# Low parts of attention keys on both partition halves, and compression products filled up with zeros to 128 rows, in a two-layer decoder trunk

## The chip, the cores and the metric

The kernel runs on one core of a Trainium2 chip, as one program. The metric is the time of one execution on the device, in microseconds (us), as the median of a few runs. Names of engines: PE is the tensor engine (PEld its weight loads), DVE the vector engine, ACT the scalar engine, POOL the general engine, SP the one that issues transfers.

## What is computed

The reference is a decoder trunk of two layers on 256 tokens of 1024 features, all in float32. Each layer is a feed-forward block, a block of token mixing, a read of a memory, and a second feed-forward block, each followed by a layer norm. Token mixing runs four mixers on one input projection; two of them, DSA and NSA, are attention of four heads of 64 channels on one shared key head:

```python
def token_mixing(x, w_in, ...):
    parts = jnp.split(x @ w_in, np.cumsum(IN_SPLITS)[:-1].tolist(), axis=-1)
    y_ret, y_dsa, y_nsa, y_ssd = retention(...), dsa_attention(...), nsa_attention(...), ssd_mixer(...)
    gates = jax.nn.sigmoid(br_g.reshape(B, S, N_BRANCH, D))
    merged = jnp.einsum('bsnd,bsnd->bsd', gates, jnp.einsum('bsnw,nwd->bsnd', ys, w_branch))
    return merged @ w_out

# in dsa_attention: one stream of keys; in nsa_attention: two (selected blocks, window)
s = jnp.einsum('bqhd,bqnd->bhqn', qb, ks) * (Dh ** -0.5)
# in nsa_attention, besides: windows of 32 tokens, every 16, compressed to one key and one value each (15 of them)
def compress(t, i):
    blk = t[:, tok] + cmp_pos[i]
    h = jax.nn.gelu(blk.reshape(B, n_cmp, CMP_LEN * Dh) @ cmp_w1[i])
    return h @ cmp_w2[i]
p_cmp = masked_softmax(jnp.einsum('bshd,bcd->bhsc', q, k_cmp) * scale, cmp_visible[None, None])
o_cmp = jnp.einsum('bhsc,bcd->bshd', p_cmp.astype(v_cmp.dtype), v_cmp)
```

## The kernel before

Products are made of two parts for accuracy. A float32 operand is split into a high part that a single pass of the tensor engine carries exactly, and a low part, the remainder; a product is then high by high, high by low and low by high. Weights stream in through SP into buffers named `raw`, ACT makes their high parts `wH` (L177), DVE their low parts `wL` (L178), and PE multiplies (L191 to L193 in `mm3`; L369 and L370 in the feed-forward blocks).

The order of the work on PE is written down by the program: the mixers are Python generators whose small steps are woven between the dense products of the projections, gates and branches (`Weave`, with a fixed rate and fixed shares). So each engine has one fixed sequence of instructions and runs it in order; what differs from run to run is only when each may start.

The attention of DSA and NSA is `attend`. Queries lie in `qT` with 128 rows: the high parts of the 64 channels on partitions 0 to 63, the low parts on 64 to 127. The keys' high parts `keyH` are there twice, on both halves, so that one product over 128 rows gives (high + low query) by high key. The keys' low parts `keyL` lie on the lower half only, and the second product takes the first 64 rows of both. Per head that is

```python
nc.tensor.matmul(r, q, self.keyH[:, kg, :nk], start=i == 0, stop=False, skip_group_check=True)           # L649
nc.tensor.matmul(r, q[:64], self.keyL[:, kg, :nk], start=False, stop=False, skip_group_check=True)       # L650
```

with `nk` = 128 keys for the first 128 queries and 256 for the second. Heads are done four at a time for 128 keys and two at a time for 256, and then one product adds the mask (L654). A maximum by DVE (L657), exponentials by ACT (L660), and a multiplication by POOL (L670) follow, and later transposes on PE (L681), a split of their result by ACT and DVE (`PT`, L207 and L208), and the products with the values (L691, L692).

The compression of NSA has four small float32 products on fewer than 128 rows: L961 (`w2r` by `gx`, rows 0 to 63), L962 (`hrep` by `w2`, rows 64 to 127), and two at L1000 (`vblk` by `pcT`, 64 rows). A float32 product shows as two passes in the trace. `shared_keys` builds `keyH` and `keyL` (L907, L908); `nsa` holds the compression.

Of the kernel before, what the change touches and what calls it, by code (L numbers as in the profile page):

```python
# [9 lines left out]
F32 = mybir.dt.float32  # L10
# [15 lines left out]
# steps of the mixers woven into the dense products, per step of those, and the mixers' shares of them  # L26
# [3 lines left out]
# columns of w_in, as the reference splits them  # L30
# [8 lines left out]
# token-major projection groups, in the order of their columns in the on-chip tile  # L39
# [11 lines left out]
# layout of the weight stream: name -> (offset, floats per partition)  # L51
# [28 lines left out]
# constants that depend on shapes alone  # L80
# [16 lines left out]
def whole(g):  # L97
    """Runs a generator to its end and returns its value."""
    while True:
        try:  # L100
            next(g)
        except StopIteration as e:
            return e.value


class Weave:
    """Weaves chains of small steps into the large products: step() takes the next step of one of them."""
# [18 lines left out]
    def over(self, g, rate):  # L126
        """Runs g, with rate steps of the chains after each of its own."""
# [11 lines left out]
class Trunk:  # L139
# [33 lines left out]
    def split(self, src, n, pool=None):  # L173
        """The exact parts of float32 weights that single-pass products carry."""
# [13 lines left out]
    def mm3(self, out, a, b, start, stop, **kw):  # L188
        """out += a.T @ b in float32 accuracy; a and b are (high, low) pairs."""
        mm = self.nc.tensor.matmul  # L190
        mm(out, a[0], b[0], start=start, stop=False, **kw)  # L191
        mm(out, a[0], b[1], start=False, stop=False, **kw)  # L192
        mm(out, a[1], b[0], start=False, stop=stop, **kw)  # L193
# [16 lines left out]
    def prime(self, g):  # L210
        """Takes a unit of products to its first yield: its weights are loaded and split."""
# [6 lines left out]
    def ahead(self, *key):  # L218
        """A unit that only prepares a chunk of weights."""
# [3 lines left out]
    def run(self, units, then=None, weave=None, rate=0):  # L223
        """Runs units of products; the weights of the next one are prepared ahead of each."""
# [8 lines left out]
    def setup(self):  # L233
# [3 lines left out]
        # the activation table and the tensor engine's clock come up while the first loads run  # L237
# [41 lines left out]
    def later(self, v):  # L279
        """Holds a load into v's tile until the products reach this point: other loads are needed sooner."""  # L280
# [12 lines left out]
    def layer_norm(self, acc, out=None, alone=False):  # L293
# [21 lines left out]
        # the transposes wait for the sums: other products go between them  # L315
        for t in range(2 if out is None else 0):
            for _ in range((2, 5)[t]):
                yield
            if t == 1 and alone:
                # with no other products the tensor engine's clock is kept up  # L320
# [13 lines left out]
    def ffn(self, l, name, wk, dn, hook=None, first=False, then=None, hold=False):  # L334
# [3 lines left out]
        def gu(f):  # L338
            early = f if first else 2
            if early < 2:  # L340
                # the first blocks follow their loads, some input features at a time
# [22 lines left out]
            # a bank each for gate and up: the products with the high parts of x beside those with its low parts  # L364
# [27 lines left out]
        # split: the first unit, for which the caller makes room ahead of the layer norm before it  # L392
# [13 lines left out]
        # the last blocks finish the token tiles one after the other  # L406
# [33 lines left out]
    def kv_unit(self, l, i):  # L440
        """Units 0-3 hold two blocks of key features each, 4-5 and 6-7 a half of the values."""
# [24 lines left out]
    def xattn(self, l, wk, dn, queries, then, apart):  # L466
# [52 lines left out]
        def out(h, n):  # L519
            # the last n heads together  # L520
# [5 lines left out]
        # with products to come under the layer norm the last heads need not finish together  # L526
# [20 lines left out]
    def token_acc(self, acc, blocks, first, last):  # L547
        """Blocks of 2 x 128 input features into all 1024 token-major columns; the last ones a token tile at a time."""
# [34 lines left out]
    def rope(self, n, heads, width, half, tab, mp):  # L583
        """Rotates the first 2 * half of each of the heads' columns, in place, for both token tiles."""
# [13 lines left out]
    def tposes(self, out, srcs, scale=None, eng="act", parts=128):  # L598
        """Up to four [128, <=128] token-major blocks, transposed side by side into out."""
# [8 lines left out]
    def stacked(self, n, mp):  # L608
        """Queries of four heads by token tiles, transposed: the high parts over the low ones."""
# [17 lines left out]
    def values(self, names, mp):  # L627
        """The parts of values by token tiles, side by side."""
# [7 lines left out]
    def attend(self, qT, streams, mask, mp, finish):  # L636
        """Causal attention of four heads on one key head, for streams of keys, values and a scale of their own that are
        added up; mask(t): further 0/1 rows of masked keys. The sums come out with the channels on the partitions."""
        nc = self.nc

        def weights(t, kg, gate, ps):
            """exp(s - max) of four heads, over the sums."""
            nk, hb = 128 * (t + 1), 4 >> t
            sums = self.sm.tile([128, 4], F32, name="s4", tag="s4", bufs=4)
            for h0 in range(0, 4, hb):
                s = self.acc()
                for i in range(hb):
                    q, r = qT[t][:, h0 + i], s[:, i * nk:i * nk + nk]
                    nc.tensor.matmul(r, q, self.keyH[:, kg, :nk], start=i == 0, stop=False, skip_group_check=True)  # L649
                    nc.tensor.matmul(r, q[:64], self.keyL[:, kg, :nk], start=False, stop=False, skip_group_check=True)  # L650
                sv = s[:, :hb * nk].rearrange("p (h k) -> p h k", h=hb)
                # without a mask only the last block of keys has any that come later
# [22 lines left out]
        def products(t, v, ps, first, last):  # L675
# [19 lines left out]
            # the products with the low parts of the values are on the upper half  # L695
# [6 lines left out]
        # the weights of each stream run ahead of the products of the one before  # L702
# [12 lines left out]
    def branch_parts(self, b, y, scale, mp, feat=False):  # L715
        """The transposed parts [128, 2, 256] of y, which is token-major [128, 2, 256] unless feat."""
        nc = self.nc
        # two branches hold their parts at a time
# [705 lines left out]
```

## Time and profile before

| | |
|---|---|
| runs | 1488.06, 1488.38 and 1484.4 us; median 1488.06 us |
| span of the profiled execution | 1484.8 us; no time of its own is recorded beside it |
| PE busy | 1468.4 us, 99% of the span |
| PE weight loads busy | 1298.8 us, 87% |
| DVE, ACT, POOL busy | 1059.2 us (71%), 801.5 us (54%), 124.2 us (8%) |
| mean granted clock of PE | 0.997 of full speed |

The span goes from the first to the last instruction of the program. Busy time is the time in which at least one instruction of the engine is shown as running; matmuls are pipelined and overlap each other in the record, so a row's duration is longer than the step from one product to the next, and it is the steps between starts that add up to the time.

### The profile page before, as it was taken

To read this page: it belongs to the slowest core of one execution; us is meant where nothing else is said; L and a number is where in the kernel's file an instruction comes from. 1 tells how busy PE (TensorE), PEld (TensorE's weight loads), DVE (VectorE), ACT (ScalarE), POOL (GpSimd) and SP (SyncE) were. 2 spreads that over 40 slices of the span, in tenths; PEclk is the share of its full clock that TensorE was granted. 3 is DMA by queue.
4 is the path that set the end of the run, shared out by engine and by line. 5 is a ranking of instruction groups with operands and counts; after the bars stand their busy time and mean duration, and the time that the engine had idled before them with its cause. 6 is when DMAs were issued, how large, how long until landed. Compare 5 with 4: busy or idle time off the path is not lost.

```text
span 1484.8 us, 22612 instructions
## 1 busy us (share of the span) xinstructions
PE 1468.4 (99%) x8949; PEld 1298.8 (87%) x8949; DVE 1059.2 (71%) x1671; ACT 801.5 (54%) x1302; POOL 124.2 (8%) x122
## 2 busy tenths in 40 slices
PE   8999999999999999999999999999999999999997
PEld 6888899899997989888898888898998989888886
DVE  7666668886668777666686566788866688676565
ACT  6555546644554646555545465466445546365552
POOL 0000002201321000000000000023013210000000
PEclk9999999999999999999999999999999999999999
DMA  8576545533345745555556555554433556264550
GB/s 311 194 276 238 185 165 170 173 140 114 117 169 183 262 149 195 202 199 198 198 173 221 193 208 185 174 189 170 143 114 115 175 192 229 100 241 171 204 192 29
DMA packets 40857, 269.38 MB, mean 181 GB/s; under 512 B 4528, under 2 KB 4784, under 8 KB 10288
## 3 DMA queue, kind: packets, MB, share of 16 engines
q1 hardware_dynamic: 40176, 266.89, 50.7%
q8 instruction: 70, 1.15, 0.3%
q10 hardware_dynamic: 576, 1.05, 0.2%
q14 instruction: 35, 0.29, 0.1%
HBM read 266.88 MB, written 1.05 MB: 180 GB/s over the span
## 4 chain that ended last, share of the span: by engine, by line
PE 96%; DVE 1%; DMA 1%; ACT 1%; POOL 0%; issue 0%; DVEq 0%; ACTq 0%
PE tp L369 11%; PE mm L369 11%; PE acc L193 10%; PE acc L191 10%; PE acc L192 10%; PE mm L191 8%; PE mm L192 8%; PE mm L193 8%; PE mm L370 5%; PE tp L370 5%; PE acc L650 1%; PE tp L327 1%; PE acc L649 1%; PE tp L192 1%; PE tp L681 1%; PE tp L193 1%
## 5 line engine op out<-in xcount | busy, mean ns | idle before, releaser
L178 DVE TENSOR_TENSOR wL<-raw,wH 128x1024 fp32r<-128x1024 f32 (+2 forms) x478 | 583.8, 1230 | 240.1 <-ACT wH L177 237.3
L177 ACT ACTIVATE wH<-raw 128x1024 fp32r<-128x1024 f32 (+2 forms) x478 | 496.1, 1048 | 306.7 <-PE mm L192 134.4
L369 PE MATMUL mm<-xP,wH 128*128 128x512 f32 x704 | 249.4, 394 | 1.7 <-DVE xP L208 1.7
L369 PE MATMUL tp<-xP,wH 128*128 128x512 f32 x704 | 249.1, 394 | 0.0
L191 PE MATMUL mm<-xP,wH 128*128 128x256 f32 x736 | 214.5, 291 | 0.3 <-ACT vM L200 0.3
L192 PE MATMUL mm<-xP,wH 128*128 128x256 f32 x736 | 209.0, 284 | 0.0
L193 PE MATMUL mm<-xP,wL 128*128 128x256 f32 x736 | 208.6, 283 | 0.0
L370 PE MATMUL mm<-xP,wL 128*128 128x256 f32 x704 | 195.7, 278 | 0.8 <-DVE wL L178 0.8
L370 PE MATMUL tp<-xP,wL 128*128 128x256 f32 x704 | 195.4, 278 | 0.0
L369 PEld LDWEIGHTS mm<-xP,wH 128*128 128x128 f32 x704 | 132.0, 187 | 33.3 <-ACT wH L177 2.0
L369 PEld LDWEIGHTS tp<-xP,wH 128*128 128x128 f32 x704 | 132.0, 188 | 30.7
L191 PEld LDWEIGHTS mm<-xP,wH 128*128 128x128 f32 x736 | 141.1, 192 | 2.4 <-ACT vM L200 1.4
L192 PEld LDWEIGHTS mm<-xP,wH 128*128 128x128 f32 x736 | 141.2, 192 | 1.3 <-issue 0.6
L193 PEld LDWEIGHTS mm<-xP,wL 128*128 128x128 f32 x736 | 141.1, 192 | 0.1
L192 PE MATMUL acc<-wL,hH 128*128 128x512 f32 x352 | 137.8, 392 | 0.0
L191 PE MATMUL acc<-wH,hH 128*128 128x512 f32 x352 | 137.7, 391 | 0.0
L193 PE MATMUL acc<-wH,hL 128*128 128x512 f32 x352 | 137.5, 391 | 0.0
L370 PEld LDWEIGHTS mm<-xP,wL 128*128 128x128 f32 x704 | 132.2, 188 | 5.3 <-DVE wL L178 1.9
L370 PEld LDWEIGHTS tp<-xP,wL 128*128 128x128 f32 x704 | 132.3, 188 | 0.0
L374 ACT ACTIVATE g<-mm 128x256 f32<-128x256 f32 x88 | 33.8, 384 | 116.6 <-PE mm L370 116.6
L375 DVE TENSOR_TENSOR g<-mm,g 128x256 f32<-128x256 f32 x88 | 37.2, 423 | 78.4 <-ACT g L374 78.3
L193 PE MATMUL acc<-wH,xP 128*128 128x512 f32 (+1 forms) x224 | 85.0, 379 | 1.9 <-POOL xP L1193 1.9
(328 smaller groups left out, 2392.6 us busy)
## 6 DMA issues: line engine op xcount, KB each, us to landing
raw<-in_w_dram SPq DMA_DIRECT2D x232, 1024.0 KB, 4.9
raw<-in_memT_dram SPq DMA_DIRECT2D x5, 1024.0 KB, 4.8
lnG<-in_ln_g_dram SPq DMA_DIRECT2D x8, 512.0 KB, 4.1
lnB<-in_ln_b_dram SPq DMA_DIRECT2D x8, 512.0 KB, 4.8
raw<-in_w_dram SPq DMA_DIRECT2D x4, 624.0 KB, 3.9
w<-in_w_dram SPq DMA_DIRECT2D x8, 256.0 KB, 5.1
raw<-in_xT_dram ACTq DMA_DIRECT2D x4, 256.0 KB, 6.3
raw<-in_w_dram SPq DMA_DIRECT2D x4, 256.0 KB, 6.0
```

The source lines that it names most:

```text
L177: self.nc.scalar.activation(h, src, AF.Copy)
L178: self.nc.vector.tensor_tensor(lo, src, h.bitcast(F32), OP.subtract)
L191: mm(out, a[0], b[0], start=start, stop=False, **kw)
L192: mm(out, a[0], b[1], start=False, stop=False, **kw)
L193: mm(out, a[1], b[0], start=False, stop=stop, **kw)
L327: nc.tensor.transpose(p[:, k * 128:k * 128 + 128], X[:, t, (h * 4 + k) * 128:(h * 4 + k + 1) * 128], self.ident)
L369: nc.tensor.matmul(b[s], w[0][:, off:off + 128], self.xP[:, :, k], start=k == 0, stop=False, skip_group_check=True)
L370: nc.tensor.matmul(b[s][:, :256], w[1][:, off:off + 128], self.xH[:, k], start=False, stop=k == 7, skip_group_check=True)
L374: nc.scalar.activation(g[:, s], b[s][:, 256:], AF.Copy)
L375: nc.vector.tensor_tensor(g[:, s], b[s][:, :256], g[:, s], OP.add)
L649: nc.tensor.matmul(r, q, self.keyH[:, kg, :nk], start=i == 0, stop=False, skip_group_check=True)
L650: nc.tensor.matmul(r, q[:64], self.keyL[:, kg, :nk], start=False, stop=False, skip_group_check=True)
```

## The change

The keys' low parts are stored on both halves of the partitions, as the high parts are, and the second product of the scores takes all 128 rows: it now gives (high + low query) by low key, which adds the tiny product of the two low parts. The four small products of the compression get operands of 128 rows, of which the half that was absent is filled with zeros by POOL. Comments are gone as well, so lines move by up to five (L957 is L960, L1000 is L1005 in the changed kernel).

```diff
 # attend
-                    nc.tensor.matmul(r, q[:64], self.keyL[:, kg, :nk], start=False, stop=False, skip_group_check=True)
+                    nc.tensor.matmul(r, q, self.keyL[:, kg, :nk], start=False, stop=False, skip_group_check=True)
...
 # shared_keys
-        self.keyL = mp.tile([64, 3, S], F32R, name="keyL", bufs=1)
+        self.keyL = mp.tile([128, 3, S], F32R, name="keyL", bufs=1)
...
-            nc.vector.tensor_tensor(self.keyL[:, sl], src[:64], self.keyH[:64, sl].bitcast(F32), OP.subtract)
+            nc.vector.tensor_tensor(self.keyL[:, sl], src, self.keyH[:, sl].bitcast(F32), OP.subtract)
...
 # nsa
         rep = self.sm.tile([128, 4, 16], F32, name="hrep", bufs=1)
+        nc.gpsimd.memset(rep[:64], 0.0)
...
-        w2r = self.sm.tile([64, 2, 64], F32, name="w2r", bufs=1)
-        nc.gpsimd.tensor_scalar(w2r, w2[:64, None, :].to_broadcast([64, 2, 64]), 0.5, None, op0=OP.mult)
+        w2r = self.sm.tile([128, 2, 64], F32, name="w2r", bufs=1)
+        nc.gpsimd.memset(w2r[64:], 0.0)
+        nc.gpsimd.tensor_scalar(w2r[:64], w2[:64, None, :].to_broadcast([64, 2, 64]), 0.5, None, op0=OP.mult)
...
-        nc.tensor.matmul(cp[0][:, :16], w2r.rearrange("p a b -> p (a b)"), x[:64, 0, :], start=True, stop=True)
-        nc.tensor.matmul(cp[1][:64, :64], rep[64:].rearrange("p a b -> p (a b)"), w2[64:], start=True, stop=True)
+        nc.tensor.matmul(cp[0][:, :16], w2r.rearrange("p a b -> p (a b)"), x[:, 0, :], start=True, stop=True)
+        nc.tensor.matmul(cp[1][:64, :64], rep.rearrange("p a b -> p (a b)"), w2, start=True, stop=True)
...
-        vb = mp.tile([64, 4, 64], F32, name="vblk", bufs=1)
+        vb = mp.tile([128, 4, 64], F32, name="vblk", bufs=1)
+        nc.gpsimd.memset(vb[64:], 0.0)
...
-        pcT = mp.tile([64, S], F32, name="pcT", tag="t2")
-        self.tposes(pcT, [pc[:, t].rearrange("p h c -> p (h c)") for t in range(2)], parts=64, eng="dve")
+        pcT = mp.tile([128, S], F32, name="pcT", tag="t2")
+        nc.gpsimd.memset(pcT[64:], 0.0)
+        self.tposes(pcT[:64], [pc[:, t].rearrange("p h c -> p (h c)") for t in range(2)], parts=64, eng="dve")
```

The sequences of PE, DVE, ACT and SP have the same instructions in the same places as before. POOL's gets eight instructions more, four in each layer. The first place is POOL's queue at the start of token mixing in the first layer, with the rotation of the index queries (`rope`); - and + are before and change.

```order
 L261 CAST lowb<-consts 128x128
-L1218 TENSOR_SCALAR cwh<-SP 128x32
-L957 TENSOR_SCALAR w2r<-SP 64x128
+L1223 TENSOR_SCALAR cwh<-SP 128x32
+L960 TENSOR_SCALAR w2r<-SP 64x128
 L307 TENSOR_TENSOR lnrs<-lnmv,mhalf 128x1 x2
+L970 MEMSET vblk 64x256
 L593 TENSOR_TENSOR rope_2170<-pj,consts 128x144
```

The zero fill of `vblk` now stands ahead of the rotation, though it is needed much later. The second place is POOL's queue where the attention weights of DSA are multiplied (`P`), with what each instruction waits for; first before.

```order
L670 TENSOR_TENSOR P<-P,rs_3638 128x512 [waits DVE_49,PE_49,Activation_49]
L670 TENSOR_TENSOR P<-P,rs_3757 128x512 [waits PE_49,DVE_49,Activation_49,Pool_49]
L670 TENSOR_TENSOR P<-P,rs_3757 128x512 [waits PE_49,Activation_49]
L1188 TENSOR_TENSOR gate<-gate 128x512 [waits DVE_49] x2
L670 TENSOR_TENSOR P<-P,rs_3967 128x512 [waits DVE_49,PE_49,Activation_49]
```

And the change:

```order
L670 TENSOR_TENSOR P<-P,rs_3641 128x512 [waits DVE_49,Activation_49]
L670 TENSOR_TENSOR P<-P,rs_3760 128x512 [waits DVE_49,PE_49,Activation_49]
L670 TENSOR_TENSOR P<-P,rs_3760 128x512 [waits PE_49,Activation_49]
L999 MEMSET pcT 64x256 [waits PE_49,Pool_49]
L1193 TENSOR_TENSOR gate<-gate 128x512 [waits DVE_49,Pool_49]
L1193 TENSOR_TENSOR gate<-gate 128x512 [waits DVE_49]
L670 TENSOR_TENSOR P<-P,rs_3971 128x512 [waits DVE_49,PE_49,Activation_49]
```

The zero fill of `pcT` stands behind three of the multiplications, and the additions to the gates stand behind it. The third place is PE's queue around the products of `vblk` and `pcT`, between dense products of a branch; first before.

```order
L193 MATMUL acc<-yH,wL 128x256
L1000 MATMUL acc<-pcT,vblk 128x256 [waits DVE_49]
L1000 MATMUL acc<-pcT,vblk 128x256
L191 MATMUL mm<-yH,wH 128x256 [waits Activation_49]
L192 MATMUL mm<-yL,wH 128x256
```

And the change:

```order
L193 MATMUL acc<-yH,wL 128x256
L1005 MATMUL acc<-pcT,vblk 128x256 [waits DVE_49,Pool_49]
L1005 MATMUL acc<-pcT,vblk 128x256
L191 MATMUL mm<-yH,wH 128x256 [waits Activation_49]
L192 MATMUL mm<-yL,wH 128x256
```

PE now waits there for POOL's zero fill as well as for DVE's copy of the transposed weights.

## Rows read from the trace of the kernel before

**Rows 1.** The page: its span, and the chain that ended last, by engine.

```profile
span 1484.8 us, 22612 instructions
...
PE 96%; DVE 1%; DMA 1%; ACT 1%; POOL 0%; issue 0%; DVEq 0%; ACTq 0%
```

**Rows 2.** Instructions of line 650: count, duration in ns, first and last start, rows*columns and forms.

```profile
L650 PE MATMUL acc<-keyL,qT x48: 322/352/382, 340.8 to 1147.3; 64*128 64x128 f32 x24, 64*128 64x256 f32 x24
```

**Rows 3.** PE in order of time, scores of 128 keys: start us, duration us, what.

```profile
340.68 0.22 PE L649 MATMUL acc<-keyH,qT 128*128 128x128 f32 x1
340.83 0.32 PE L650 MATMUL acc<-keyL,qT 64*128 64x128 f32 x1
...
342.62 0.39 PE L654 MATMUL acc<-bm,nident 128*128 128x512 bf16 x1
...
342.96 0.28 PE L192 MATMUL mm<-xP,wH 128*128 128x256 f32 x1
```

**Rows 4.** PE in order of time, scores of 256 keys.

```profile
390.10 0.28 PE L649 MATMUL acc<-keyH,qT 128*128 128x256 f32 x1
...
391.25 0.28 PE L654 MATMUL acc<-cmb,nident 128*128 128x256 bf16 x1
...
391.49 0.28 PE L192 MATMUL mm<-xP,wH 128*128 128x256 f32 x1
391.61 0.28 PE L193 MATMUL mm<-xP,wL 128*128 128x256 f32 x1
```

**Rows 5.** PE in order of time, products of 128 rows and 128 columns elsewhere.

```profile
249.19 0.45 PE L603 MATMUL tp<-identr,iqp 128*128 128x128 f32 x4
...
249.67 0.28 PE L192 MATMUL mm<-xP,wH 128*128 128x256 f32 x1
...
252.41 0.33 PE L850 MATMUL acc<-ikT,iqT 128*128 128x128 f32 x2
252.59 0.67 PE L1090 MATMUL acc<-sA,ones 128*128 128x512 f32 x2
```

**Rows 6.** PE in order of time, float32 products: of 128 rows, and of 64.

```profile
278.13 1.02 PE L1113 MATMUL acc<-xc,xc 128*128 128x256 f32 x4
...
366.26 1.13 PE L1000 MATMUL acc<-pcT,vblk 64*128 64x256 f32 x4
...
367.54 0.28 PE L192 MATMUL mm<-yL,wH 128*128 128x256 f32 x1
```

**Rows 7.** Weight loads for the scores in order of time.

```profile
340.56 0.19 PEld L649 LDWEIGHTS acc<-keyH,qT 128*128 128x128 f32 x1
340.83 0.18 PEld L650 LDWEIGHTS acc<-keyL,qT 64*128 64x128 f32 x1
```

**Rows 8.** ACT, DVE and PE in order of time, around the last value products.

```profile
403.54 1.06 ACT L177 ACTIVATE wH<-raw 128x1024 fp32r<-128x1024 f32 x1 [1.99 <-PE mm L192]
...
410.51 0.68 DVE L208 TENSOR_TENSOR PT<-tp,PT 128x512 fp32r<-128x512 f32 x1
...
411.93 0.39 PE L692 MATMUL acc<-PT,vp 128*64 128x512 f32 x1
```

**Rows 9.** POOL in order of time, with its idle time before in brackets.

```profile
223.33 0.54 POOL L593 TENSOR_TENSOR rope<-pj,consts 128x144 f32<-128x144 f32 x1 [28.46 <-ACT pj L200]
...
360.86 2.04 POOL L670 TENSOR_TENSOR P<-P,rs 128x512 f32<-128x512 f32 x2 [10.63 <-DVE rs L666]
```

**Rows 10.** A stretch of the first layer: busy us of PE, PEld, DVE, ACT, POOL, then the clock.

```profile
350.30:353.70 3.40, 3.40 (x18) 3.40 (x17) 1.04 (x4) 0.76 (x1) 0.00 (x0) 0.50 0.00 0
```

**Rows 11.** PE in order of time: the same two places in each layer.

```profile
348.52 1.85 PE L975 MATMUL acc<-kcT,qT 128*128 128x16 f32 x16
...
355.15 0.28 PE L649 MATMUL acc<-keyH,qT 128*128 128x256 f32 x1
...
1093.12 1.85 PE L975 MATMUL acc<-kcT,qT 128*128 128x16 f32 x16
...
1098.21 0.28 PE L649 MATMUL acc<-keyH,qT 128*128 128x256 f32 x1
```

More of the change, by code (lines that the diff above doesn't have):

```diff
@@ L960, in nsa @@
         cp = [self.acc() for _ in range(2)]
-        nc.tensor.matmul(cp[0][:, :16], w2r.rearrange("p a b -> p (a b)"), x[:64, 0, :], start=True, stop=True)
-        nc.tensor.matmul(cp[1][:64, :64], rep[64:].rearrange("p a b -> p (a b)"), w2[64:], start=True, stop=True)
+        nc.tensor.matmul(cp[0][:, :16], w2r.rearrange("p a b -> p (a b)"), x[:, 0, :], start=True, stop=True)
+        nc.tensor.matmul(cp[1][:64, :64], rep.rearrange("p a b -> p (a b)"), w2, start=True, stop=True)
         kcT = self.sm.tile([128, 16], F32, name="kcT", bufs=1)
         nc.scalar.activation(kcT, cp[0][:, :16], AF.Copy)
-        vb = mp.tile([64, 4, 64], F32, name="vblk", bufs=1)
+        vb = mp.tile([128, 4, 64], F32, name="vblk", bufs=1)
+        nc.gpsimd.memset(vb[64:], 0.0)
         bm = self.c("blkm", 64)
-        nc.vector.tensor_tensor(vb, cp[1][:64, None, :64].to_broadcast([64, 4, 64]), bm[:, :, None].to_broadcast([64, 4, 64]), OP.mult)
+        nc.vector.tensor_tensor(vb[:64], cp[1][:64, None, :64].to_broadcast([64, 4, 64]), bm[:, :, None].to_broadcast([64, 4, 64]), OP.mult)
         yield
```

## The prediction

> **What bounds the kernel now.** I read the page first. Its chain of work that ended last is PE for 96% of a span of 1484.8 us [rows 1], so what PE's queue no longer needs comes off the end, as long as PE finds its operands ready. The list of waits names no wait of PE in either attention stage that is longer than a fraction of a microsecond; PE runs there without a gap. So the second view is PE in order of time, and in it the step from one start to the next, since a row's duration overlaps the next one's.
>
> In that view the second product of the scores stands out. There are 48 of them, 24 with 128 columns and 24 with 256, all on 64 rows [rows 2]. With 128 keys, the seven steps from the first of them to the mask take 342.62 - 340.83 = 1.79 us, 0.256 each, whichever of the two kinds follows [rows 3]. Elsewhere two products of 128 rows and 128 columns follow each other at (252.59 - 252.41) / 2 = 0.09 us, and four more with a dense one behind them take 249.67 - 249.19 = 0.48 us [rows 5]. With 256 keys, the four products take 391.25 - 390.10 = 1.15 us, 0.29 each [rows 4], where a dense product of the same 128 rows and 256 columns takes 391.61 - 391.49 = 0.12 us. The weight loads say why: the load for L649 that follows a dense product starts at 340.56, 0.12 us ahead of its product at 340.68, while the load for L650 starts at 340.83, together with its product [rows 3, 7]. A load that goes ahead is hidden; one that waits for the array to be empty is not. This happens in both directions, from 128 rows to 64 and back, so both products of a pair pay.
>
> The Trainium skill has this as a rule: "TensorEngine Tiling (Array Packing)", section Tiling Modes, says that changing the tiling mode drains the engine, and that merely changing the tile doesn't. The rows agree with it, as far as they go. The same skill has a rule that speaks against the change: "TensorE: Matmul & The Clock Gate", section LDWEIGHTS, says that a weight load takes as long for few rows as for all 128, since the columns set its time. The two loads agree with that too, at 0.18 and 0.19 us [rows 7]; by that rule alone the rows of a product would cost nothing and the time would stay, which is a rival below.
>
> **The change part by part.** PE's instructions, their order and their columns stay; what goes is the change of rows between neighbours.
>
> *Scores of 128 keys*: three groups of eight products and a mask in each layer, six in all. From the first product to the second dense one behind the mask a group takes 342.96 - 340.68 = 2.28 us [rows 3]. The part from the mask on, 342.96 - 342.62 = 0.34, stays. The eight products, if they go as the two rows of their own shape do, take 8 x 0.09 = 0.72 us [rows 5]. So 2.28 - 0.34 - 0.72 = 1.22 us a group, **7.3 us**. At the dense step of 256 columns, 0.12, which they can hardly exceed with half of the columns, it would be 0.98 a group, 5.9 us; at half of that step, 0.06, it would be 1.46, 8.8 us. I take the middle, since rows of exactly this shape show it.
>
> *Scores of 256 keys*: six half groups of four products in each layer, twelve in all. One takes 391.49 - 390.10 = 1.39 us up to the second dense product, of which 391.49 - 391.25 = 0.24 stay [rows 4]. Four at 0.12 are 0.48, so 1.39 - 0.24 - 0.48 = 0.67 each, **8.0 us**. With the dense step between 0.115 and 0.125 it is 7.8 to 8.3.
>
> *Compression*: the two products of L1000 make four passes, which with the dense product behind them take 367.54 - 366.26 = 1.28 us; four float32 passes of 128 rows and the same columns are 1.02 us from the first start to the last end, against 1.13 here [rows 6]. So streaming is nearly the same, and what can go is the way in and the way out, some 0.2 to 0.4 us. I take 0.3 us for each layer, and 0.2 for the smaller pair L961 and L962, which has two such changes of shape: **1.0 us** in all, between 0 and 1.6.
>
> *What is added.* DVE's subtraction for `keyL` runs over twice the partitions with the same elements on each; the price of that lies between nothing and a doubling of two instructions a layer, and I take nothing, since DVE is idle for 29% of the span. POOL gets eight zero fills. Its rows of comparable size are the multiplications of 128x512 at 1.02 us each [rows 9]; none of the fills is larger, so the eight cost POOL 8 us at the most and probably a quarter. POOL is idle for 92% of the span, so the question is only who waits. The fill of `vblk` stands ahead of the rotation of the index queries, for which POOL had been idle for 28.46 us [rows 9]; it needs only memory that the feed-forward block used, long free by then. The fill of `pcT` stands behind three multiplications that end at 360.86 + 2.04 = 362.90; even at 1.02 us it would be through at 363.92, and PE comes to L1000 at 366.26 [rows 6, 9]: 2.3 us of cover. Behind it in POOL's queue stand additions to gates, which come 8 us later. So nothing here, and if that cover were gone each microsecond of lateness would be one of PE's.
>
> *What is late next.* PE is to run ahead by about 8 us in each layer, so others must keep pace. The tightest hand-over is the value products: PE comes to L692 at 411.93, and the low part that it needs was ready at 410.51 + 0.68 = 411.19, 0.74 us before [rows 8]. ACT, which makes the high part first, had been busy almost without a gap since 403.54, about when PE began a half group (a pair of L649 and L650) that will be 0.67 us shorter. So that cover falls to about 0.1 us. Other hand-overs of this kind have their chain begin behind the last shortened group and move along with PE. I put **0.3 us** a layer for new waits, 0.6 in all, between 0 and 4.
>
> *The clock.* For 3.4 us of the first layer the granted clock was 0.50, that is 1.2 instead of 2.4 GHz [rows 10]. Ahead of it stood the slow scores of 256 keys and then sixteen products of 16 columns at 348.52. From there to the next scores the first layer takes 355.15 - 348.52 = 6.63 us and the second, which shows no drop, 1098.21 - 1093.12 = 5.09 us for the same instructions [rows 11], so the drop costs 1.5 us. With the scores done faster, PE is better filled ahead of that place. I put 6 in 10 on the drop not coming back, and take the **1.5 us**.
>
> The sum: 7.3 + 8.0 + 1.0 - 0.6 + 1.5 = 17.2 us off the profiled span of 1484.8, which is 1467.6. The median of the runs is 1488.06 - 1484.8 = 3.3 us above that span. With it the forecast is **1471 us**, 1.2% below the median.
>
> **The rivals.**
>
> *The waits eat half of it.* If ACT and DVE are late by 0.5 us at each of the nine value products of a layer, that is 18 x 0.5 = 9 us of the 17, and the time is 1480 us. For it: the cover of 0.74 us at one of them, and that both engines work in bursts there. Against it: ACT is busy for 54% of the span, DVE for 71%, and PE shows no wait in these stages now.
>
> *The rows were not the cause.* The pairs also have in common that both products load the same queries and add into the same bank. If that, and not the rows, makes the 0.256 us, then the rule on weight loads holds alone and the time stays at 1488 us. Against it: the feed-forward and dense products add into one bank too and go at 0.12, and the load that starts late is always at a change of rows.
>
> *The zero fill stops PE.* PE's wait at L1005 is new, and it hangs on POOL, whose three multiplications ahead of the fill wait for DVE's reciprocals [rows 9]. If the fill ended later than 366.26 - 2.6 = 363.7 us (by then PE is 2.6 us ahead, from one group and two half groups), PE would wait; to lose the whole gain of some 8.5 us in the layer it would have to end 8.5 us beyond that, at 372.2. At 375 in each layer the kernel would take 1488 + 2 x 2.8 = 1494 us. Against it: POOL is through with the multiplications at 362.90, which themselves move ahead with PE.
>
> **How the numbers follow.** I give the forecast 0.81, the waits that eat half 0.12, the rows that were not the cause 0.04, and the zero fill 0.03. By itself the forecast ranges from 1466 (upper bounds of the groups, 1.7 us more; runs near the lowest of 1484.4 before, 3.7 less) to 1477 (lower bounds of the two scores and of the compression, 2.6 us; drop of the clock stays, 1.5; waits, 2). With the waits that eat half, and a run or two from the lower end, the range is 1464 to 1481 us. What a measurement of this kernel can tell from no change is about 0.3%, 4.5 us. Faster by more than that are the first two cases, 0.93; the same is the third, 0.04; slower is the last, 0.03.
>
> **What would show it.** In the changed kernel's trace L650 is to read 128*128, its weight load is to start ahead of its product, and the steps are to be 0.06 to 0.12 us for 128 keys and 0.12 for 256. A group of 128 keys is to take about 1.1 us from its first product to the second dense one behind the mask, a half group of 256 keys about 0.7. The list of waits should show PE waiting at L691 or L692 for less than 1 us a layer, and at L1005 not at all. The stretch behind the sixteen small products should have a clock of 1.00. The prediction is wrong if the steps stay at 0.25 us, which would acquit the rows, or if the steps shrink and PE's idle time grows by as much.

## The result and the profile after

The changed kernel takes 1469.99 us, the median of four runs (1469.61 to 1470.56); the kernel before takes 1487.43 us (four runs: the three of the table above and 1486.8). The ratio is 0.9888 [0.9876, 0.99]: 1.1% faster. The profiled execution took 1470.16 us for a span of 1468.4 us, so 1.8 us lie around the span.

The page of the changed kernel, as in [rows 1], with the busy time of the engines:

```profile
span 1468.4 us, 22627 instructions
...
PE 1451.9 (99%) x8949; PEld 1292.0 (88%) x8949; DVE 1059.1 (72%) x1671; ACT 800.4 (55%) x1302; POOL 126.1 (9%) x130
...
PE 96%; DVE 1%; DMA 1%; ACT 1%; POOL 0%; issue 0%; DVEq 0%; ACTq 0%
```

The span is 16.4 us shorter and the chain is still PE's for 96%: PE stayed the bound, and its queue got shorter. The 48 low products, which answer to [rows 2] (count, duration in ns, first and last start, form):

```profile
L650 PE MATMUL acc<-keyL,qT x48: 273/277/281, 340.7 to 1130.7; 128*128 128x128 f32 x24, 128*128 128x256 f32 x24
```

They have 128 rows now. The last of them started at 1147.3 before and starts at 1130.7 now, the first at 340.8 and 340.7. So 16.5 us are gained between the first and the last. Matched start by start, PE is ahead by 9.0 us at the end of the first layer's attention stage, by 9.35 at the start of the second's, and by 16.8 at its end; 0.4 us of that is lost again behind PE's last product. Next, PE in order of time (start us, duration us, what): a group of 128 keys, a half group of 256 keys and the float32 products, as in [rows 3, 4, 6].

```profile
340.65 0.22 PE L649 MATMUL acc<-keyH,qT 128*128 128x128 f32 x1
340.71 0.27 PE L650 MATMUL acc<-keyL,qT 128*128 128x128 f32 x1
340.82 0.28 PE L649 MATMUL acc<-keyH,qT 128*128 128x128 f32 x1
340.94 0.28 PE L650 MATMUL acc<-keyL,qT 128*128 128x128 f32 x1
...
341.50 0.39 PE L654 MATMUL acc<-bm,nident 128*128 128x512 bf16 x1
...
341.84 0.28 PE L192 MATMUL mm<-xP,wH 128*128 128x256 f32 x1
...
362.17 1.02 PE L1005 MATMUL acc<-pcT,vblk 128*128 128x256 f32 x4
...
363.15 0.28 PE L192 MATMUL mm<-yL,wH 128*128 128x256 f32 x1
...
383.76 0.28 PE L649 MATMUL acc<-keyH,qT 128*128 128x256 f32 x1
...
384.24 0.28 PE L654 MATMUL acc<-cmb,nident 128*128 128x256 bf16 x1
...
384.48 0.28 PE L192 MATMUL mm<-xP,wH 128*128 128x256 f32 x1
```

A group of 128 keys takes 341.84 - 340.65 = 1.19 us, where it took 2.28; a half group 384.48 - 383.76 = 0.72 us instead of 1.39; the products of `pcT` 363.15 - 362.17 = 0.98 instead of 1.28. The weight loads, as in [rows 7]:

```profile
340.54 0.19 PEld L649 LDWEIGHTS acc<-keyH,qT 128*128 128x128 f32 x1
340.66 0.19 PEld L650 LDWEIGHTS acc<-keyL,qT 128*128 128x128 f32 x1
```

The load for L650 starts at 340.66, 0.05 us ahead of its product and 0.01 us behind the start of L649; before, it started only with its product, 0.15 us behind L649. It takes as long as it did.

The stretch that stood at half clock in [rows 10], and the two starts of [rows 11] in the first layer (PE in order of time):

```profile
350.30:353.70 3.40, 3.40 (x30) 3.33 (x29) 2.77 (x8) 2.94 (x8) 0.00 (x0) 1.00 0.22 29
```

```profile
346.74 1.85 PE L979 MATMUL acc<-kcT,qT 128*128 128x16 f32 x16
...
351.83 0.28 PE L649 MATMUL acc<-keyH,qT 128*128 128x256 f32 x1
```

The clock is 1.00 there, and from the sixteen small products to the next scores the layer takes 351.83 - 346.74 = 5.09 us, exactly what the second layer took before.

Last, the zero fill of `pcT` on POOL and the one new wait, in PE's weight loads (in order of time, the wait in brackets):

```profile
357.87 1.04 POOL L670 TENSOR_TENSOR P<-P,rs 128x512 f32<-128x512 f32 x1
358.97 0.31 POOL L999 MEMSET pcT<- 64x256 f32 x1
```

```profile
383.47 0.13 PEld L692 LDWEIGHTS acc<-PT,vp 128*64 128x64 f32 x1 [0.33 <-DVE PT L208]
```

The fill ends at 359.28, 2.9 us before L1005. The wait stands once in each layer, at another of the nine value products than the one that the prediction had named.

### The profile page after: what moved, and what is told of

Same layout as the page of the kernel before. It is cut to its first block, busy times and chain, and to the rows that moved or that the text cites. A ratio compares the mean times of both kernels' runs of the same rounds, so it can differ in the third digit from the quotient of the medians.

```text
span 1468.4 us, 22627 instructions
## 1 busy us (share of the span) xinstructions
PE 1451.9 (99%) x8949; PEld 1292.0 (88%) x8949; DVE 1059.1 (72%) x1671; ACT 800.4 (55%) x1302; POOL 126.1 (9%) x130
## 4 chain that ended last, share of the span: by engine, by line
PE 96%; DVE 1%; DMA 1%; ACT 1%; POOL 0%; issue 0%; DVEq 0%; ACTq 0%
PE tp L369 11%; PE mm L369 11%; PE acc L193 10%; PE acc L191 10%; PE acc L192 10%; PE mm L191 8%; PE mm L192 8%; PE mm L193 8%; PE mm L370 5%; PE tp L370 5%; PE tp L327 1%; PE tp L192 1%; PE tp L681 1%; PE tp L193 1%; PE tp L191 1%; PE tp L603 1%
## 5 line engine op out<-in xcount | busy, mean ns | idle before, releaser
L369 PE MATMUL mm<-xP,wH 128*128 128x512 f32 x704 | 249.4, 394 | 1.8 <-DVE xP L208 1.8
L369 PE MATMUL tp<-xP,wH 128*128 128x512 f32 x704 | 249.1, 394 | 0.0
L191 PE MATMUL mm<-xP,wH 128*128 128x256 f32 x736 | 213.9, 291 | 0.3 <-ACT vM L200 0.3
L193 PE MATMUL mm<-xP,wL 128*128 128x256 f32 x736 | 208.0, 283 | 0.0
L370 PE MATMUL mm<-xP,wL 128*128 128x256 f32 x704 | 195.7, 278 | 0.5 <-DVE wL L178 0.5
L370 PE MATMUL tp<-xP,wL 128*128 128x256 f32 x704 | 195.4, 278 | 0.0
L369 PEld LDWEIGHTS mm<-xP,wH 128*128 128x128 f32 x704 | 132.0, 187 | 33.6 <-ACT wH L177 2.5
L369 PEld LDWEIGHTS tp<-xP,wH 128*128 128x128 f32 x704 | 132.0, 188 | 30.7
L191 PEld LDWEIGHTS mm<-xP,wH 128*128 128x128 f32 x736 | 140.6, 191 | 2.3 <-ACT vM L200 1.4
L193 PEld LDWEIGHTS mm<-xP,wL 128*128 128x128 f32 x736 | 140.6, 191 | 0.1
L191 PE MATMUL acc<-wH,hH 128*128 128x512 f32 x352 | 137.7, 391 | 0.0
L193 PE MATMUL acc<-wH,hL 128*128 128x512 f32 x352 | 137.5, 391 | 0.0
L370 PEld LDWEIGHTS mm<-xP,wL 128*128 128x128 f32 x704 | 132.3, 188 | 5.0 <-DVE wL L178 1.6
L370 PEld LDWEIGHTS tp<-xP,wL 128*128 128x128 f32 x704 | 132.3, 188 | 0.0
L193 PE MATMUL acc<-wH,xP 128*128 128x512 f32 (+1 forms) x224 | 85.0, 379 | 1.9 <-POOL xP L1198 1.9
```

The source lines that it names most:

```text
L369: nc.tensor.matmul(b[s], w[0][:, off:off + 128], self.xP[:, :, k], start=k == 0, stop=False, skip_group_check=True)
L370: nc.tensor.matmul(b[s][:, :256], w[1][:, off:off + 128], self.xH[:, k], start=False, stop=k == 7, skip_group_check=True)
```

## The experiments

The theory: the array has to run empty whenever a product has other rows than the one before it, and the steps of 0.25 to 0.29 us are that. Its rivals: each product of 64 rows is slow by itself; the two products of a pair are slow because they share their queries and their bank; the gain comes from the compression or the clock. All times are medians; the kernel before ran between them on the same chip (1488.11 us for the first four, 1486.92 for the next four, 1488.26 for the last three).

**Each half of the change alone.** The first kernel is the one before with the scores changed, the second is the changed one with the scores put back (`keyL` and its subtraction go along in both; the cuts show the product alone).

```
 e1, against the kernel before
-                    nc.tensor.matmul(r, q[:64], self.keyL[:, kg, :nk], start=False, stop=False, ...)
+                    nc.tensor.matmul(r, q, self.keyL[:, kg, :nk], start=False, stop=False, ...)
 e2, against the changed kernel
-                    nc.tensor.matmul(r, q, self.keyL[:, kg, :nk], start=False, stop=False, ...)
+                    nc.tensor.matmul(r, q[:64], self.keyL[:, kg, :nk], start=False, stop=False, ...)
```

> Only the scores take 128 rows; the compression products keep their 64 rows and POOL has no zero fills. If the change of rows between neighbours is the price and the scores hold nearly all of it: 1471 us, that is the changed kernel plus 1.0 for the compression, with L650 in steps of 0.11 to 0.12 us and no stretch of half clock in the first layer. If the compression products or what hangs on them (the clock behind them) brought the gain: 1480 us or more.

> Only the compression products are filled up to 128 rows; the scores keep 64 rows for the low parts. By the change of rows: 1.0 us below the kernel before, about 1486.4 us, not to be told from it by its time; in the trace the four passes of vblk and pcT with the dense product behind them take 0.98 instead of 1.28 us, and the scores still step by 0.25 and 0.29. By the rival that the compression brought the gain: 1475 us or less. Whether a stretch of half clock shows behind the sixteen small products tells if the slow scores are needed for it.

The scores alone take 1470.44 us (1469.18 to 1472.87), ratio 0.9892 [0.9874, 0.991]; the compression alone takes 1486.25 us in ten runs (1482.99 to 1488.6), ratio 0.9994 [0.9982, 1.0005]. The scores hold the gain. The first kernel's trace has no stretch at half clock in either attention stage; the second keeps the stretch at half clock, behind its slow scores and the small products (columns as in [rows 10], the clock is the figure third from the end):

```profile
351.00:354.40 3.40, 3.40 (x19) 3.40 (x19) 1.29 (x5) 1.39 (x3) 0.00 (x0) 0.56 0.00 0
```

**Fewer changes of rows, with all 48 products of 64 rows kept.** All high products of a group go first, then all low ones, which have 64 rows as before.

```
                 for i in range(hb):
                     q, r = qT[t][:, h0 + i], s[:, i * nk:i * nk + nk]
                     nc.tensor.matmul(r, q, self.keyH[:, kg, :nk], start=i == 0, stop=False, ...)
-                    nc.tensor.matmul(r, q, self.keyL[:, kg, :nk], start=False, stop=False, ...)
+                for i in range(hb):
+                    q, r = qT[t][:, h0 + i], s[:, i * nk:i * nk + nk]
+                    nc.tensor.matmul(r, q[:64], self.keyL[:64, kg, :nk], start=False, stop=False, ...)
```

> As the changed kernel, but the low parts of the keys again over 64 rows, and in each group all products with the high parts first, then all with the low parts: as many 64-row products as before, but two changes of rows in a group instead of eight (four in a half group). If each change of rows costs 0.14 to 0.17 us: 6 x 2 x 0.14 + 12 x 2 x 0.17 = 5.7 us above the changed kernel, 1476 us, and steps between two 64-row products of 0.12 us or less. If a 64-row product is slow by itself: nearly the whole gain is lost, 1485 us or more. If neighbours that load the same queries were slow: 1470 us, since no such neighbours are left.

It took 1474.75 us (1474.72 to 1476.6), ratio 0.9922 [0.9906, 0.9938], its span 1472.9 us. The same group of 128 keys, PE in order of time:

```profile
340.99 0.56 PE L649 MATMUL acc<-keyH,qT 128*128 128x128 f32 x4
341.48 0.66 PE L652 MATMUL acc<-keyL,qT 64*128 64x128 f32 x4
342.07 0.39 PE L656 MATMUL acc<-bm,nident 128*128 128x512 bf16 x1
...
342.41 0.28 PE L192 MATMUL mm<-xP,wH 128*128 128x256 f32 x1
```

The group takes 342.41 - 340.99 = 1.42 us, against 1.19 with 128 rows throughout and 2.28 with the rows changed at every product. There are as many products of 64 rows as before the change, and they are no longer slow; two changes of rows are left in each group and half group, 36 in all, and the span is 1472.9 - 1468.4 = 4.5 us above the changed kernel's (expected: 5.7): 0.125 us for each change. Where rows changed at every product it had been 1.09 / 8 = 0.14 us with 128 keys and 0.67 / 4 = 0.17 with 256. So it is the change of rows that costs, not the 64 rows. Here the queries of neighbours differ, which by itself speaks for the rival of shared queries as well, but the changed kernel shares them and is at 0.11 a step: that rival is out.

The Trainium skill, "TensorEngine Tiling (Array Packing)", section Tiling Modes, has the rule: changing the tiling mode drains the engine. The traces agree, and put the price at 0.12 to 0.17 us per change in this stream. The next kernel looks at columns.

**All 128 columns too.** The value products L692 (64 columns of weights, between neighbours with 128) and the compression product L965 get 128 columns; the added ones go into rows of PSUM that nobody reads.

```
-                nc.tensor.matmul(o[:64], v[:, j, :64], pT[1], start=False, stop=last and j == t, ...)
+                nc.tensor.matmul(o, v[:, j], pT[1], start=False, stop=last and j == t, ...)
...
-        nc.tensor.matmul(cp[1][:64, :64], rep.rearrange("p a b -> p (a b)"), w2, start=True, stop=True)
+        nc.tensor.matmul(cp[1][:, :64], rep.rearrange("p a b -> p (a b)"), w2, start=True, stop=True)
```

> As the changed kernel, but the 18 value products that fill 64 of the 128 columns (L692) and the small product of L965 take all 128 columns; of the value products this adds the tiny product of the low parts. If only a change of rows has a price: the time of the changed kernel, 1470 us, and steps of 0.23 us around L692 as before. If a change of columns had the price of a change of rows, some 0.15 us each way: 18 x 2 x 0.15 = 5.4 us less, 1464.6 us. The step of 0.19 us into L965 may fall to 0.11, which is 0.2 us a layer and not to be seen in the time.

It took 1469.69 us (1469.37 to 1473.66), ratio 0.9895 [0.9875, 0.9914], no other than the changed kernel. The eighteen L692 show no price, with 512 streamed columns each: in the changed kernel, too, their step is 0.23 us, and the weight load goes ahead by as much (load at 360.32, product at 360.54), though its columns differ from its neighbours'. The small float32 product L965 does show one. With 64 columns its load starts together with it (334.76), and in the second layer the way from L964 to the second dense product takes 1070.51 - 1069.74 = 0.77 us; with 128 columns the load goes ahead, and the same way takes 1069.80 - 1069.16 = 0.64. That is 0.13 us for the change of columns in and out, too little for the time to show. What sets the two places apart was not tested. By the time, what to align between neighbours in this kernel is rows.

**The slow scores put back at one place.** 64 rows for the low products of the 256-key half groups of DSA alone: two half groups in each layer, eight products in all. One of the two stands directly ahead of the sixteen small products.

```
                     nc.tensor.matmul(r, q, self.keyH[:, kg, :nk], start=i == 0, stop=False, ...)
-                    nc.tensor.matmul(r, q, self.keyL[:, kg, :nk], start=False, stop=False, ...)
+                    n = 64 if mask and t == 1 else 128
+                    nc.tensor.matmul(r, q[:n], self.keyL[:n, kg, :nk], start=False, stop=False, ...)
```

> As the changed kernel, but the low parts over 64 rows again for the 256-key scores of DSA alone, which stand right ahead of the sixteen small products. Two half groups in each layer cost 4 x 0.67 = 2.7 us: 1472.7 us. If the slow scores ahead of the small products make the stretch of half clock, it comes back and costs 1.5 us more in one or each layer: 1474 to 1476 us. If the clock fell for another reason, it stays at 1.00 there.

Its four runs are 1472.69, 1473.49, 1474.42 and 1478.03 us; median 1473.95, ratio 0.9911 [0.9892, 0.9929]. The profiled one is the 1478.03, and it has three stretches at half clock, two of them behind the small products, one in each layer (columns as in [rows 10]):

```profile
349.70:353.10 3.40, 3.40 (x18) 3.40 (x18) 1.13 (x6) 1.19 (x2) 0.69 (x1) 0.52 0.00 0
445.30:448.70 3.40, 3.40 (x9) 2.68 (x10) 3.40 (x5) 1.08 (x2) 1.28 (x1) 0.53 0.03 7
1090.40:1093.80 3.40, 3.40 (x19) 3.40 (x18) 1.72 (x4) 2.38 (x7) 0.05 (x1) 0.52 0.00 0
```

The drop behind the small products follows the slow scores: it is there in this kernel, in the one with the compression alone and in the kernel before, and in no profile of a kernel whose scores ahead of the small products are all of 128 rows, nor in that of the kernel with the low products in a row. The four slow half groups by themselves are worth 4 x 0.67 = 2.7 us, which puts the kernel at 1472.7 us, where its lowest run lies; the profiled run stands 5.3 us above that with its three stretches. So the drops do not come in each run: of the four, only the profiled one has a mean clock of 0.997 or less. Such a clock stands beside 20 of the 27 runs of the kernel before in these experiments and 8 of the 10 with the compression alone, and beside one of the 29 runs of kernels whose scores have 128 rows throughout (without the twenty-four fills below), though a single stretch can hide in 0.998, as with the eight fills. What it is in the slow scores that brings the clock down was not tested. That one stretch lies at 445.3, where PE had waited 1.46 us at the start of the output products, shows that slow scores are not the only way to it; the changed kernel has the same wait, and no drop.

**The zero fill made longer.** The fill of `pcT` is done eight times over in one kernel and twenty-four times in another, which the cut shows.

```
-        nc.gpsimd.memset(pcT[64:], 0.0)
+        for _ in range(24):
+            nc.gpsimd.memset(pcT[64:], 0.0)
```

> As the changed kernel, but the zero fill of pcT is made eight times in a row, so that it ends some 2 us later. In the changed kernel it ends at 359.3 us and PE comes to L1005 at 362.2, so by the cover that the prediction counts on no wait shows there and the time stays at 1470 us. If the fill were already the last thing that PE waits for there: 4 us more.

> The zero fill of pcT is made 24 times in a row and ends some 6.9 us later, past PE's arrival by 4 us. By the rival's mechanism PE waits for POOL at L1005 for about 4 us in each layer: 1478 us, more if the clock falls to half in the wait. If PE does not wait for the fill in truth: 1470 us.

Eight fills took 1472.22 us in the one run, and PE doesn't wait: the fills run from 359.38 for 2.86 us, to 362.24, and L1006 (L1005 in the changed kernel) starts at 362.58. The 2 us are not POOL's: PE loses them between 439 and 444 us, where the trace has a stretch at half clock from about 443 us that the changed kernel's has not. So eight fills are just covered, as reckoned. Twenty-four took 1477.96 us (1475.42 to 1479.24), ratio 0.9939 [0.9923, 0.9955]. POOL and PE in order of time:

```profile
359.12 8.68 POOL L1000 MEMSET pcT<- 64x256 f32 x24
```

```profile
364.77 0.28 PE L191 MATMUL mm<-yH,wH 128*128 128x256 f32 x1
367.85 2.07 PE L1006 MATMUL acc<-pcT,vblk 128*128 128x256 f32 x4 [2.80 <-POOL pcT L1000]
```

PE waits 2.8 us in each layer for POOL, less than the 4 expected, since in this kernel the order of PE's queue puts 22 more dense products ahead of L1006. The four passes behind the wait take 2.07 us in the first layer and 1.67 in the second, instead of 1.02: around the end of the wait the clock falls to half, in both layers. The kernel loses 8.0 us, of which the two waits are 5.6. So the rival in which the zero fill stops PE is a real mechanism, with a cover of 2.9 us that holds in the changed kernel.

**A further step: the small products in one pass.** The compressed scores are sixteen float32 passes of 16 columns, in 1.85 us. With `kcT` as a high and a low half side by side, eight fp32r products of 32 columns do, and DVE adds the halves; nothing is left out.

```
-        kcT = self.sm.tile([128, 16], F32, name="kcT", bufs=1)
-        nc.scalar.activation(kcT, cp[0][:, :16], AF.Copy)
+        kcT = self.sm.tile([128, 2, 16], F32R, name="kcT", bufs=1)
+        self.hl_from(kcT[:, 0], kcT[:, 1], cp[0][:, :16])
...
-                nc.tensor.matmul(sc[:, c:c + 16], nqT[t][:, h].bitcast(F32), kcT, start=True, stop=True)
+                nc.tensor.matmul(sc[:, c:c + 32], nqT[t][:, h], kcT.rearrange("p a c -> p (a c)"), start=True, stop=True)
```

> As the changed kernel, but each of the eight score products against the compressed keys is one single-pass product over 32 columns, the keys' high and low parts side by side, whose halves DVE adds, instead of a float32 product of two passes over 16 columns. In the changed kernel sixteen passes take 1.8 us a layer, 0.11 each, as the 128-column products do, so it seems that the weight load sets the step; then eight of them take 0.9 us, the time falls by 1.8 us to about 1468 us, and no run shows half clock behind them. If the columns or the passes set the step otherwise: 1470 us.

It took 1474.71 us (1474.0 to 1475.38), ratio 0.992 [0.9905, 0.9934]: slower than the changed kernel by 4.7 us, a miss. The place itself did what was expected (PE in order of time):

```profile
348.27 1.15 PE L979 MATMUL acc<-kcT,qT 128*128 128x32 f32 x8
349.27 0.36 PE L191 MATMUL mm<-xP,wH 128*128 128x256 f32 x1
```

It takes 1.00 us; the sixteen passes took 348.44 - 346.74 = 1.70 by the same two starts. But the feed-forward blocks had become slower, which the edit doesn't touch. What it does move is memory: `kcT` is 64 bytes a partition longer, and every tile that is laid out behind it begins 64 bytes later; the operands of L369 and L370, the first products of those blocks, lie ahead of it. Three kernels tell that apart: the same with an unused tile that makes the shift 256 bytes, the changed kernel with an unused tile of 64 bytes and no other edit, and the changed kernel once more.

```
 e10: n = 48, against e9; e11: n = 16, against the changed kernel
+        pad = self.sm.tile([128, n], F32, name="pad", bufs=1)
+        nc.gpsimd.memset(pad[:, :1], 0.0)
```

> As the run with one-pass compressed scores, which took 1474.7 us though its small products took 0.8 us a layer less, but with an unused tile of 192 bytes on each partition behind the longer kcT, so that all later tiles lie 256 bytes further than in the changed kernel instead of 64. In the slower run the feed-forward products stepped by 236 instead of 232 ns and 117 instead of 113 although their own operands lay where they did before. If the shift of the later tiles by 64 bytes did that: 1468 us and steps of 232 and 113 again. If something else in the one-pass form did: 1474 to 1475 us.

> The changed kernel with nothing but an unused tile of 64 bytes on each partition at the same place, so that all later tiles lie 64 bytes further, as in the slower run. If the shift makes the feed-forward products slower: 1470 + 4.5 + 1.7 = 1476 us, steps of 236 and 117. If not: 1470 us.

> The changed kernel itself, beside the two runs with moved tiles on the same chip: 1470 us, steps of 232 and 113, by every theory but one: if chips differ in these steps, it takes what the slower run took, 1474 us or more.

| kernel | median us (runs) | ratio to before | span us |
|---|---|---|---|
| changed, again | 1469.3 (1468.88 to 1471.13) | 0.9883 [0.9867, 0.99] | 1467.7 |
| changed, tiles shifted by 64 bytes | 1476.83 (1476.21 to 1477.35) | 0.9931 [0.9916, 0.9946] | 1475.1 |
| one pass, tiles shifted by 256 bytes | 1467.82 (1467.49 to 1471.06) | 0.9875 [0.986, 0.9891] | 1466.1 |

The shift of 64 bytes alone costs 1475.1 - 1467.7 = 7.4 us. First the changed kernel, then the shifted one: the same two instructions of the first feed-forward block, 340 steps from the first start to the second, and the group of line 369 (instructions, busy us and mean ns, idle time).

```profile
97.55 0.40 PE L369 MATMUL mm<-xP,wH 128*128 128x512 f32 x1
...
161.87 0.40 PE L369 MATMUL mm<-xP,wH 128*128 128x512 f32 x1
```

```profile
L369 PE MATMUL mm<-xP,wH 128*128 128x512 f32 x704 | 249.5, 395 | 1.9 <-DVE xP L208 1.7
```

```profile
98.03 0.40 PE L369 MATMUL mm<-xP,wH 128*128 128x512 f32 x1
...
163.11 0.40 PE L369 MATMUL mm<-xP,wH 128*128 128x512 f32 x1
```

```profile
L369 PE MATMUL mm<-xP,wH 128*128 128x512 f32 x704 | 253.6, 399 | 1.6 <-DVE xP L208 1.6
```

The stretch takes 65.08 us instead of 64.32, with no wait that is longer. Each product of line 369 is some 4 ns longer, and the loss is spread over the first products of the feed-forward blocks: over the whole kernel the 1408 steps of line 369 take 5.2 us more and the 1408 of line 370 2.3 us more, 3.7 and 1.6 ns each, while the blocks' second products (L191 to L193) step at 229 ns in both kernels. With the shift at 256 bytes it is gone, and the one-pass kernel's span is 1.6 us below that of the changed kernel run beside it, about the two layers' 2 x 0.7. It is the fastest kernel by its median, 1467.82 us, though its interval and that of the changed kernel overlap. Why 64 bytes cost and 256 don't was not found out: which tile has to lie where was not tried. The gain of the change itself is not of this kind: its larger tiles take more partitions, not more bytes on each, so that no tile begins elsewhere, and PE comes to the first scores, behind the whole first feed-forward block, at 340.68 us before and 340.65 after.

## Why the prediction held, by its own steps

The forecast was 1471 us (1464 to 1481), the measurement 1469.99.

- **What bounds the kernel** was read rightly. What PE's queue lost came off the end: the terms measured below sum to 16.6 us, the span fell by 16.4.
- **Scores of 128 keys**: the mechanism was right, the size off. Predicted 1.06 us a group at 0.09 a step, measured 1.19, since the steps are 0.11 (340.71, 340.82, 340.94), only the first is 0.06. That is 1.09 saved instead of 1.22, 6.5 us over six groups instead of 7.3, inside the bounds of 5.9 to 8.8. The 0.09 came from a pair [rows 5] that is too short to show the pace of a run of eight; the sixteen passes of 16 columns in the trace of before (1.85 us, [rows 11]) had shown 0.11 for each new load of weights, and were the better row.
- **Scores of 256 keys**: predicted 0.72 us a half group, measured 0.72; 8.0 us, as forecast.
- **Compression**: 0.30 us a layer at `pcT` as forecast, and 0.09 more on the way in. I had put 0.2 on L964 and L965; they take 0.77 us up to the second dense product where the pair took 0.80, and with another 0.09 on the way in it is 0.12. About 1 us in all; the kernel with the compression alone can't be told from before.
- **What is added**: DVE's larger subtractions (414 to 684 ns, before 403 to 675) and the zero fills cost nothing that PE sees. A fill of `pcT` takes 0.31 us (estimated: up to 1.02) and ends at 359.28, where the rival needed an end behind 363.7; eight fills did not make PE wait, twenty-four did.
- **New waits**: 0.33 us in each layer at an L692, of which its step, 0.40 us instead of 0.23 to 0.24, shows 0.17 on PE, and the step behind it 0.05 more. Predicted 0.3 a layer; about 0.4 in all instead of 0.6. The place was not the one named. The rival in which the waits eat half would have needed 0.5 us at all nine.
- **The clock**: the drop did not come back, 1.5 us as forecast at 6 in 10, and with the slow scores put back it came back in both layers of the profiled run, though not in each run. The reason given, that PE is better filled ahead of that place, was not tested by itself.
- **From the span to the median**: the sum gave a span of 1467.6 us, measured 1468.4; on top I had put the 3.3 us by which the median of before stood above its profiled span. In every run with both numbers the own time is the span and 1.8 us, so the other 1.5 us were something else. The runs of before lie at about 1484.3, 1486.8 and 1488.5 us, which go with mean clocks of 0.999, 0.997 and 0.996, and the profiled one (0.997, a span of 1484.8) has one stretch at half clock in the middle: I take it that the runs at 1488.5 have two, one in each layer, and those at 1484.3 none, but none of these was profiled. By that reading the median of before held a second drop, which the change removed as well, and of the 17.4 us between the medians some 3 are the clock's. The term was too large by 1.5 and the span too short by 0.8; that the two offset each other in part, so that the forecast came out within 1 us, is luck.

The rival that the rows were not the cause fell with the load of L650 that goes ahead now, and with the kernel that keeps the 64 rows but not the changes.

## What to carry to other kernels

Look at the steps between starts, not at durations, wherever products of different row counts alternate: a weight load that starts together with its product, not ahead of it, and waits for no other engine marks the place, and either filling up to equal rows (with zeros or, as the keys here, with a second copy) or sorting the products by rows takes most of the price away. Filling is the better one as long as the columns stay and the fill has cover; compare the fill's end with the first reader. And when an edit makes an untouched stage slower, look at what it did to the addresses before explaining it by the engines.

## What the runs showed of the hardware that was not expected

A change between 64 and 128 rows costs 0.12 to 0.17 us in a stream of fp32r products, while eighteen products of 64 columns between products of 128 showed no price; at one small float32 product a change of columns and back cost 0.13 us. Products that stream 128 columns and each load new weights go at 0.11 us, no slower than those that stream 16. Small products behind slow scores, or a wait of 1.5 to 2.8 us, can be followed by 3.4 us at half clock, at about 1.5 us each; behind the small products PE is shown as busy throughout. And a shift of later tiles by 64 bytes a partition cost 7.4 us, 3.7 ns for each product of line 369 and 1.6 for each of line 370, while one of 256 bytes, in the kernel with the one-pass products, cost nothing.
